# First feed-forward by seven products per pair of weight tiles on mixed halves of two token streams, and the long-convolution filters built in the mixers

## The chip, the cores and the metric

One NeuronCore of one Trainium2 chip runs the whole layer in one launch. The metric is the device time of a run in microseconds (us). The five engines have a queue each and run it in order: TensorE (PE, its weight loads are PEld), VectorE (DVE), ScalarE (ACT), GpSimd (POOL) and SyncE (SP, which here only starts DMAs). A scheduler fixes the order of each queue when the program is built, so an instruction that waits holds up everything behind it on its engine.

## The reference

A diffusion-transformer layer over 512 latent tokens (`x`) and 256 context tokens (`ctx`), width 1024, cut to what matters:

```python
h = half_ffn(h, m[0], m[1], m[2], wg0, wu0, wd0)        # 512 tokens, D_FF = 2816 = 22 tiles of 128
hc = half_ffn(hc, mc[0], mc[1], mc[2], wg0, wu0, wd0)   # 256 tokens, the same weights
n, nc = modulate(rms_norm(h), ...), modulate(rms_norm(hc), ...)
s_fw, s_bw = context_states(nc, w_in, lb)               # gated linear recurrence, final states
out = token_mixers(n, s_fw, s_bw, hyena_kernels(...))   # recurrence heads + long convolutions, gates, w_out
h = half_ffn(h + m[5] * out, m[6], m[7], m[8], wg1, wu1, wd1)
return rms_norm(h) * final_norm_w

def half_ffn(h, shift, scale, gate, wg, wu, wd):
    x = modulate(rms_norm(h), shift, scale)
    return h + 0.5 * gate * ((silu(x @ wg) * (x @ wu)) @ wd)
```

`hyena_kernels` is a small network that makes the filters of the two long convolutions from weights alone. All is float32.

## The kernel before

Tokens lie along the free axis, features on the 128 partitions. A float32 product is three products of halves: `split` (L115) writes a rounded copy `hi` on ACT (L116) and the rest `lo` on DVE (L117), and `mm3` (L242) issues `whi*xhi`, `whi*xlo`, `wlo*xhi` (L244, L245, L247). Weights come as tiles of 128x1024 through three `wraw` buffers on SP's queue and are split into rings `whi` and `wlo` of three buffers each.

**Stage 1, first feed-forward** (`ffn0`, L745). Over four groups of the 22 hidden tiles, each gate or value tile is multiplied with 512 latent columns (`ps_gl`) and 258 context columns (`ps_gc`, two of them carry the shift vectors); then `down` (L443) adds the group's share into the residuals `hl` and `hc`, which stay in SBUF. Two other pieces of work are woven in: `mod_steps` (dot products for the modulation vectors on DVE, their 56 weight tiles `wmod` fetched on POOL's queue) and, through the planner `Clock`, `filters` (L627), which builds the convolution filters with POOL, DVE, ACT and a few products (`ps_w`, `ps_last`, `ps_l`, `ps_k`) and leaves them in `k_dram`.

**Stage 2, mixers.** A list `todo` of 52 pieces of plain projection work is the filler: 12 `hy` (convolution inputs), 4 `g`, 16 `m` (gates), 4 `v`, 12 `z` (inputs of the four recurrence heads) and 4 `pb`, on PE named `ps_w`, `ps_wc`, `ps_v`, `ps_pb`. `Clock.run` steps through a chain of work and, where by its cost model the chain waits on vector work, puts in filler. Chains are `convs` (L1017: four passes, two convolutions by two channel halves, products `ps_e`, `ps_i`, `ps_j` between long sequences of DVE sums and products at L1031) and `head` (L1133: four recurrence heads, two at a time, products `ps_s` and DVE work at L1176 to L1188).

```python
def allowed(f):
    if f[0] == "z":
        return f[1] == 0 or (state["conv"] and f[1] - state["heads"] < 3)
...
ck.run([convs()], fill, lambda i: True)
state["conv"] = True
```

**Stage 3** multiplies by `w_pa` and `w_out`. **Stage 4**, the second feed-forward, forms the gates and values of hidden tiles 4 to 21 pair by pair with seven products of half tiles (`pair_products`, L1350; `ps_p`, 256 columns each) on sums of weight quarters made by `quads` (L176).

Of the kernel before, what the change touches and what calls it, by code (L numbers as in the profile page):

```python
# [10 lines left out]
F32 = mybir.dt.float32  # L11
# [11 lines left out]
T = L + C  # L23
D = 1024
# [3 lines left out]
GROUPS0 = ((0, 6), (6, 12), (12, 17), (17, 22))  # L28
# [53 lines left out]

@with_exitstack
def layer_kernel(ctx: ExitStack, tc: tile.TileContext, a: dict, out: bass.AP):
# [3 lines left out]
    const = ctx.enter_context(tc.tile_pool(name="const", bufs=1))  # L88
    wp = ctx.enter_context(tc.tile_pool(name="wp", bufs=1))
    mx = ctx.enter_context(tc.tile_pool(name="mx", bufs=1))  # L90
    psp = ctx.enter_context(tc.tile_pool(name="psp", bufs=1, space=PSUM))
# [5 lines left out]
    def c8(name, dims, dt=F32):  # L97
        return mx.tile([P] + dims, dt, tag="c8", name=name, bufs=8)
# [7 lines left out]
    def c1(name, dims, dt=F32):  # L106
        return mx.tile([P] + dims, dt, tag="c1", name=name, bufs=7)
# [15 lines left out]
    RING, ONE8, TWO4, QUAD = range(4)  # L123
    hold = lambda x, kinds: [y + (k,) for y, k in zip(x, kinds)]
    plan = []
    for g, (f0, f1) in enumerate(GROUPS0):
        gu = [(a[w][0, ft], 1024) for ft in range(f0, f1) for w in ("wg", "wu")]
        plan += hold(gu[:6], [RING] * 3 + [ONE8] + [TWO4] * 2) + gu[6:] if g == 0 else gu
        down = [(a["wd"][0, dm, :, f0 * P:f1 * P], (f1 - f0) * P) for dm in range(KT)]
        plan += hold(down, [ONE8] * 3 + [RING] * 5) + down[3:6] if g == len(GROUPS0) - 1 else down  # L130
# [27 lines left out]
    def choose():  # L158
        f = next(f for f in todo if allowed(f))
# [47 lines left out]

    def prefetch(ahead=2):
        while wstate["next"] < len(plan) and sum(2 if len(h) == 2 else 1 for h in wstate["held"]) < 2 * ahead:
# [8 lines left out]
            src, cols, *kind = plan[wstate["next"]] or choose()  # L218
            if kind == [QUAD]:
                wstate["quads"] = quads(src, cols)  # L220
                continue
# [3 lines left out]
            if kind == [ONE8]:  # L225
                both = c8("wkeep", [2, 1024], F32R)
                hi, lo = both[:, 0], both[:, 1]
            elif kind == [TWO4]:
# [51 lines left out]
    nhi = const.tile([P, KT, L], F32R, name="nhi")  # L280
    nlo = const.tile([P, KT, L], F32R, name="nlo")

# [36 lines left out]
    junk = c8("junk", [2048])  # L319

    def dot(raw, i, res):
        return V.scalar_tensor_tensor(out=junk[:, 0:1024], in0=raw, scalar=1.0, in1=cvb[:, i], op0=ALU.mult, op1=ALU.mult,  # L322
                               accum_out=res)

    def mod_steps():
        pair = c8("wmod", [2, 1024])
        raw = [pair[:, 0], pair[:, 1], c4("wmod", [1024])]
# [1215 lines left out]
```

## Time and profile before

| | us |
|---|---|
| median of 3 runs (1528.41 to 1530.3) | 1530.17 |
| the profiled execution's own time | 1527.99 |
| its span, first to last instruction | 1526.2 |
| PE busy in the span | 1484.9 |
| DVE busy | 1035.7 |
| ACT busy | 555.7 |
| POOL busy | 305.7 |

Busy time is that in which at least one instruction of an engine is under way. Matmuls overlap in the pipeline, so what one costs is the step from one start to the next, not its own duration. By the starts of its products, stage 1 lasts until 655 us of the span, the convolutions lie between 730 and 884, the heads between 888 and 1078, and stage 4 goes from 1152 to the end.

### The profile page before, as it was taken

How to read it: one execution, taken by the hardware profiler on the slowest of the kernel's cores; microseconds unless marked ns; L12 is line 12 of the kernel's file. 1: busy time of each engine (PE TensorE's matmuls, PEld its weight loads, DVE VectorE, ACT ScalarE, POOL GpSimd, SP SyncE). 2: the span in 40 equal slices, each digit the busy share in tenths (PEclk: the TensorE clock that was granted, in tenths of full speed). 3: DMA queues.
4: the chain of work that ended last, by engine and by line, in shares of the span. 5: the costliest groups of instructions: out<-in, count | busy, mean ns of one | idle time of the engine just before them, and what ended most of it. 6: DMA issues, size and time to landing. Idle time of an engine off the chain costs nothing. (4 is left out here: it accounts for less than half of the span.)

```text
span 1526.2 us, 22141 instructions
## 1 busy us (share of the span) xinstructions
PE 1484.9 (97%) x8776; PEld 1294.7 (85%) x8776; DVE 1035.7 (68%) x1553; ACT 555.7 (36%) x947; POOL 305.7 (20%) x248
## 2 busy tenths in 40 slices
PE   8899999999999999999999999999998999999997
PEld 5698888888888888878888888888798889999896
DVE  7946984475456554675776756875757768769686
ACT  5342112212322232444433324444433435435253
POOL 1400110010254464000000021223431002212020
PEclk9999999999999999999999999999999999999999
DMA  8334674462223333334542421124633142332422
GB/s 333 129 108 135 200 237 148 143 233 94 80 94 99 99 107 99 132 111 138 171 137 93 131 90 49 63 90 152 218 111 94 39 128 85 96 110 88 121 83 84
DMA packets 69704, 188.93 MB, mean 124 GB/s; under 512 B 7835, under 2 KB 16799, under 8 KB 69344
## 3 DMA queue, kind: packets, MB, share of 16 engines
q1 hardware_dynamic: 58608, 152.61, 30.5%
q0 software_dynamic: 9408, 33.70, 6.7%
q8 instruction: 69, 1.13, 0.3%
q10 hardware_dynamic: 1584, 1.20, 0.2%
q14 instruction: 35, 0.29, 0.1%
HBM read 169.92 MB, written 17.56 MB: 123 GB/s over the span
## 5 line engine op out<-in xcount | busy, mean ns | idle before, releaser
L116 ACT CAST whi<-wraw 128x1024 fp32r<-128x1024 f32 (+3 forms) x188 | 171.0, 910 | 489.4 <-PE ps_gc L245 178.5
L117 DVE TENSOR_TENSOR wlo<-wraw,whi 128x1024 fp32r<-128x1024 f32 (+3 forms) x136 | 156.6, 1152 | 138.7 <-ACT whi L116 138.4
L244 PE MATMUL ps_gl<-nhi,whi 128*128 128x512 f32 x360 | 144.5, 401 | 0.0
L244 PE MATMUL ps_w<-nhi,whi 128*128 128x512 f32 x352 | 143.2, 407 | 1.3 <-ACT th L940 1.1
L247 PE MATMUL ps_w<-nhi,wlo 128*128 128x512 f32 x352 | 140.0, 398 | 3.3 <-DVE wlo L117 3.3
L247 PE MATMUL ps_gl<-nhi,wlo 128*128 128x512 f32 x360 | 142.5, 396 | 0.0
L245 PE MATMUL ps_gl<-nlo,whi 128*128 128x512 f32 x360 | 142.1, 395 | 0.0
L245 PE MATMUL ps_w<-nlo,whi 128*128 128x512 f32 x352 | 140.0, 398 | 0.0
L117 POOL TENSOR_TENSOR wlo<-wraw,whi 128x1024 fp32r<-128x1024 f32 x25 | 62.5, 2501 | 383.0 <-ACT whi L116 370.3
L245 PE MATMUL ps_dl<-mid,whi 128*128 128x512 f32 (+1 forms) x321 | 123.7, 386 | 0.0
L247 PE MATMUL ps_dl<-mid,wlo 128*128 128x512 f32 (+1 forms) x321 | 123.6, 387 | 0.0
L244 PE MATMUL ps_dl<-mid,whi 128*128 128x512 f32 (+1 forms) x321 | 123.3, 389 | 0.0
L322 DVE SCALAR_TENSOR_TENSOR junk<-wmod,cvb 128x1024 f32<-128x1024 f32 x80 | 97.7, 1222 | 2.8 <-DMA wmod<-in_mod_w 1.6
L244 PE MATMUL ps_gc<-chi,whi 128*128 128x258 f32 x328 | 93.2, 284 | 5.9 <-ACT chi L116 5.7
L245 PE MATMUL ps_gc<-clo,whi 128*128 128x258 f32 x328 | 94.0, 287 | 0.0
L247 PE MATMUL ps_gc<-chi,wlo 128*128 128x258 f32 x328 | 92.8, 283 | 0.0
L1369 POOL TENSOR_TENSOR u<-p,res 128x512 f32<-128x512 f32 x18 | 33.2, 1847 | 283.7 <-ACT p L1364 140.0
L244 PEld LDWEIGHTS ps_gl<-nhi,whi 128*128 128x128 f32 x360 | 67.5, 187 | 18.5 <-ACT bias L798 0.8
L247 PEld LDWEIGHTS ps_w<-nhi,wlo 128*128 128x128 f32 x352 | 66.5, 189 | 17.5 <-DVE wlo L117 3.7
L244 PEld LDWEIGHTS ps_w<-nhi,whi 128*128 128x128 f32 x352 | 66.7, 190 | 16.3 <-ACT th L940 1.4
L244 PEld LDWEIGHTS ps_gc<-chi,whi 128*128 128x128 f32 x328 | 62.4, 190 | 19.9 <-ACT chi L116 6.2
L332 POOL DMA_DIRECT2D wmod<-in_mod_w x56 | 29.6, 529 | 238.1 <-DVE junk L322 194.6
(460 smaller groups left out, 4102.8 us busy)
## 6 DMA issues: line engine op xcount, KB each, us to landing
wmod<-in_mod_w POOLq DMA_DIRECT2D x56, 512.0 KB, 4.5
wraw<-in_wg SPq DMA_DIRECT2D x44, 512.0 KB, 3.5
wraw<-in_wu SPq DMA_DIRECT2D x44, 512.0 KB, 3.6
wraw<-in_w_in SPq DMA_DIRECT2D x44, 512.0 KB, 3.2
wraw<-in_wd SPq DMA_DIRECT2D x40, 384.0 KB, 3.5
wm<-in_mod_w SPq DMA_DIRECT2D x16, 512.0 KB, 8.0
wraw<-in_wd SPq DMA_DIRECT2D x19, 320.0 KB, 3.3
win<-in_win SPq DMA_DIRECT2D x16, 256.0 KB, 3.4
```

The lines of the kernel that those rows point to most:

```text
L116: A.copy(hi, x)
L117: return eng.tensor_tensor(out=lo, in0=x, in1=hi.bitcast(F32), op=ALU.subtract)
L244: PE.matmul(o, whi, xhi, start=first, stop=False)
L245: PE.matmul(o, whi, xlo, start=False, stop=False)
L247: PE.matmul(o, wlo, xhi, start=False, stop=last)
L322: return V.scalar_tensor_tensor(out=junk[:, 0:1024], in0=raw, scalar=1.0, in1=cvb[:, i], op0=ALU.mult, op1=ALU.mult, accum_out=res)
L332: nc.gpsimd.dma_start(out=raw[i % 3], in_=a["mod_w"][8 * tiles[i][0] + tiles[i][1]])
L1369: G.tensor_tensor(out=u57, in0=p57, in1=res[:, 1:2].broadcast_to([P, 2, 256]), op=ALU.add)
```

## The change

Hidden tiles 4 to 21 of the first feed-forward are taken in pairs. The 1024 input features are cut into two halves, each weight pair into quarters, and the 512 latent and 256 context tokens are cut into halves too: one half of both streams, with one column for the shift and one of zeros, is a block of `HW` = 386 columns. Seven products of a quarter sum with a block or a sum of blocks (`product0`, named `ps_p`, four input tiles by three products by 386 columns) replace the eight of the plain scheme. `token_sums` makes the sums of blocks once; `quads0` makes the weight sums for each pair, and three of the seven halves get their `lo` by an accumulating DMA on POOL's queue that adds the weights from DRAM to a negated `hi`. `pair_products0` puts the results together with two ACT copies, one ACT negation, four DVE sums and three POOL sums.

There are five groups instead of four. The input blocks and their sums take the room of the residuals, so the residuals lie in DRAM: `hl` is stored in `x0_dram`, the shares of the groups are copied out of PSUM by ACT and added up in `y_dram` and `yc_dram` (a store for the first group, accumulating DMAs on POOL's queue for the next three), and the last group loads both again. `mod_steps` fetches through two buffers on SP's queue instead of three on POOL's, and dots the latent vector of the first 24 tiles in two halves. The filter network and `filters` run in stage 2, in front of the convolutions, with the mixers' pieces as filler; no `z` piece is allowed before the convolutions are done. POOL's descriptor ring is 4096 bytes of a partition.

```diff
-GROUPS0 = ((0, 6), (6, 12), (12, 17), (17, 22))
+GROUPS0 = ((0, 4), (4, 8), (8, 12), (12, 16), (16, 22))
...
-        return mx.tile([P] + dims, dt, tag="c8", name=name, bufs=8)
+        whole = mx.tile([P, 2080], dt, tag="c8", name=name, bufs=12)
...
         if f[0] == "z":
-            return f[1] == 0 or (state["conv"] and f[1] - state["heads"] < 3)
+            return state["conv"] and f[1] - state["heads"] < 3
...
+        def both(x, src=None):
+            w = ("whi", "wlo")[wstate["slot"]]
+            wstate["slot"] ^= 1
+            t = wp.tile([P, 2, 512], F32R, tag=w, name=w, bufs=3)
+            if src is None:
+                split(t[:, 0], t[:, 1], x)
+            else:
+                A.copy(t[:, 0], x)
+                A.activation(t[:, 1], t[:, 0].bitcast(F32), AF.Copy, scale=-1.0)
+                nc.gpsimd.dma_start(out=t[:, 1], in_=src, accum_op=ALU.add)
+            return t[:, 0], t[:, 1], None
+
+        yield both(a11, src0[:, 0:512])
+        s1 = total(a21, a22)
+        s2 = total(s1, a11)
+        yield both(s2)
+        yield both(total(a11, a21))
+        yield both(s1)
+        yield both(a12, src0[:, 512:1024])
+        yield both(a22, src1[:, 512:1024])
+        yield both(total(a12, s2))
...
-        raw = [pair[:, 0], pair[:, 1], c4("wmod", [1024])]
+        raw = [c4("wmod", [1024]) for _ in range(2)]
...
-                nc.gpsimd.dma_start(out=raw[i % 3], in_=a["mod_w"][8 * tiles[i][0] + tiles[i][1]])
+                load(raw[i % 2], a["mod_w"][8 * tiles[i][0] + tiles[i][1]])
...
+    def product0(name, x):
+        whi, wlo, _ = weights()
+        p_ = ps(name)
+        for k in range(4):
+            ks = slice(k * P, k * P + P)
+            mm3([p_[:, 0:HW]], whi[:, ks], wlo[:, ks], [x[k]], k == 0, k == 3)
+        return p_[:, 0:HW - 1]
...
+        p1, u2, p7, n5 = (c2(x, [n]) for x in ("p1", "u2", "p7", "n5"))
+        A.copy(p1, product0("ps_p1", [xone(k, 0) for k in range(4)]))
+        V.tensor_tensor(out=u2, in0=product0("ps_p6", tsum[1]), in1=p1, op=ALU.add)
+        A.copy(p7, product0("ps_p7", tsum[2]))
+        G.tensor_tensor(out=res[:, 1, 0], in0=p7, in1=u2, op=ALU.add)
+        A.activation(n5, product0("ps_p5", tsum[0]), AF.Copy, scale=-1.0)
...
                     down(weights(), [x + y for x, y in zip(lx, cx)], [pl, pc[:, 0:C]])
-                    residual(hl, dm, LS, pl, m_lat, 2)
-                    residual(hc, dm, CS_, pc[:, 0:C], m_ctx, 2)
+                    for p_, al, y, n in ((pl, c2, y_dram, L), (pc, c1, yc_dram, C)):
+                        t = al("yt", [n])
+                        A.copy(t, p_[:, 0:n])
+                        if gi == 0:
+                            store(y[:, dm], t)
+                        else:
+                            nc.gpsimd.dma_start(out=y[:, dm], in_=t, accum_op=ALU.add)
                     adv(bg, 2)
...
-    while "net" not in state:
-        ck.fill(fill)
-    ck.run([filters()], fill, lambda i: True)
...
     ck.run([context_norm()], fill, lambda i: True)
     ftab = forward_table()
+    ck.run([filters()], fill, lambda i: True)
     inverse_table(0)
```

The order of the queues at three places. First PE at the first pass of the convolutions, before, behind the pass's last forward product (`ps_e`; `ps_w` is a projection of the filler):

```order
L244 MATMUL ps_e<-zhi,ft 128x256
L245 MATMUL ps_e<-zlo,ft 128x256
L247 MATMUL ps_e<-zhi,ft 128x256
L247 MATMUL ps_w<-nhi,wlo 128x512
L244 MATMUL ps_w<-nhi,whi 128x512
L245 MATMUL ps_w<-nlo,whi 128x512
```

The same place in the changed program:

```order
L316 MATMUL ps_e<-zhi,ft 128x256
L317 MATMUL ps_e<-zlo,ft 128x256
L319 MATMUL ps_e<-zhi,ft 128x256
L316 MATMUL ps_i<-ys,it 128x256 x2
L316 MATMUL ps_e<-zhi,ft 128x256
L317 MATMUL ps_e<-zlo,ft 128x256
```

Before, 130 products of the filler stand between the first pass's forward and inverse products; in the changed program none does. There, 2 inverse products (`ps_i`), 19 forward ones of the next pass, 22 inverse and 5 forward ones follow; the first `ps_w` comes after the fourth pass's forward products, and 46 of them stand ahead of the last `ps_j`.

Second DVE at the same place, before, from the sums of the first pass on (`y`, `x` and `sb` are its operands, `kt` the filter):

```order
L1031 TENSOR_TENSOR y<-x,kt 128x512 x2
L1031 TENSOR_TENSOR x<-x,kt 128x512 x2
L117 TENSOR_TENSOR wlo<-wraw,whi 128x1024
L1031 TENSOR_TENSOR y<-y,x 128x256 x4
L1031 TENSOR_TENSOR x<-y 128x512
```

And in the changed program:

```order
L1225 TENSOR_TENSOR y<-x,kt 128x512 x2
L1225 TENSOR_TENSOR x<-x,kt 128x512 x2
L1225 TENSOR_TENSOR y<-y,x 128x256 x4
L1225 TENSOR_TENSOR x<-y 128x512
L1225 TENSOR_TENSOR x<-sb,x 128x512
```

The splits of filler weights (`wlo`) are gone from here; DVE has the four passes' own work one behind the other.

Third POOL in stage 1 of the changed program, at the end of the second group (`whi` and `wlo` from `in_wg` and `in_wu` are the accumulated weight halves, `g` is a result of seven products); before, POOL's queue held only the 56 `wmod` fetches and the filters' sums here:

```order
L993 DMA y_dram<-yt 128x512 x4
L993 DMA yc_dram<-yt 128x256
L262 DMA wlo<-in_wg 128x512
L262 DMA whi<-in_wg 128x512
L262 DMA wlo<-in_wu 128x512
L889 TENSOR_TENSOR g<-p_2439,u_2438 128x385
L891 TENSOR_TENSOR g<-u_2438,n_2440 128x385
L892 TENSOR_TENSOR g<-n_2440,g 128x385
L262 DMA wlo<-in_wu 128x512
```

Weight halves now stand in one queue behind the additions to `y_dram`, which wait for ACT's copies out of PSUM, and behind the sums of results, which wait for products.

## Rows read from the trace of the kernel before

**Rows 1.** The page's busy times over the whole span (us, share, instructions).
```profile
PE 1484.9 (97%) x8776; PEld 1294.7 (85%) x8776; DVE 1035.7 (68%) x1553; ACT 555.7 (36%) x947; POOL 305.7 (20%) x248
```
**Rows 2.** Windows: from:to, length, PE, PEld, DVE, ACT, POOL busy (instructions), PEclk, DMA share, GB/s.
```profile
80.00:360.00 280.00, 279.81 (x1627) 245.78 (x1626) 182.16 (x302) 66.18 (x117) 29.62 (x56) 1.00 0.52 170
400.00:580.00 180.00, 180.00 (x1010) 150.65 (x1009) 100.31 (x133) 51.36 (x94) 94.75 (x92) 1.00 0.28 90
730.00:884.30 154.30, 153.19 (x801) 129.82 (x800) 113.02 (x186) 52.69 (x77) 2.39 (x1) 1.00 0.41 135
884.30:888.50 4.20, 4.20 (x21) 3.38 (x20) 1.13 (x2) 1.42 (x2) 0.29 (x1) 1.00 0.18 68
888.50:1048.90 160.40, 156.87 (x953) 137.76 (x951) 120.90 (x193) 73.71 (x142) 40.53 (x17) 1.00 0.23 78
1048.90:1078.30 29.40, 29.22 (x155) 24.46 (x156) 13.03 (x21) 12.49 (x28) 8.80 (x4) 1.00 0.65 224
1207.00:1490.00 283.00, 279.15 (x1954) 261.20 (x1953) 220.44 (x299) 126.09 (x205) 51.44 (x36) 1.00 0.33 100
```
**Rows 3.** PE's timeline in stage 1 (start, duration, engine, line, op, tiles, form, count).
```profile
201.01 0.39 PE L244 MATMUL ps_gl<-nhi,whi 128*128 128x512 f32 x1
201.24 0.40 PE L245 MATMUL ps_gl<-nlo,whi 128*128 128x512 f32 x1
201.47 0.28 PE L244 MATMUL ps_gc<-chi,whi 128*128 128x258 f32 x1
...
202.07 0.40 PE L244 MATMUL ps_gl<-nhi,whi 128*128 128x512 f32 x1
```
**Rows 4.** PE's timeline in stage 4, seven-product part, twelve steps apart.
```profile
1310.03 0.28 PE L244 MATMUL ps_p<-nhi,wlo 128*128 128x256 f32 x1
...
1311.47 0.28 PE L244 MATMUL ps_p<-nhi,whi 128*128 128x256 f32 x1
```
**Rows 5.** Groups of DVE between 730 and 884.3 (count, busy us, mean ns, idle before).
```profile
L117 DVE TENSOR_TENSOR wlo<-wraw,whi 128x1024 fp32r<-128x1024 f32 x19 | 23.2, 1223 | 10.4 <-ACT whi L116 10.2
...
L1031 DVE TENSOR_TENSOR x<-ps_e,sb 128x512 f32<-128x512 f32 (+1 forms) x12 | 6.8, 598 | 7.9 <-PE ps_e L247 7.8
...
L1119 DVE TENSOR_TENSOR x2v<-ps_j,x2v 128x256 f32<-128x256 f32 x6 | 3.5, 626 | 12.2 <-PE ps_j L247 12.2
...
L1100 DVE TENSOR_TENSOR x1v<-ps_i,x1v 128x512 f32<-128x512 f32 x4 | 2.8, 692 | 8.3 <-PE ps_i L247 8.3
...
L942 DVE TENSOR_SCALAR KR<-th,lb_n,lbt 128x512 f32<-128x512 f32 (+1 forms) x4 | 1.6, 475 | 0.0
...
L1142 DVE TENSOR_TENSOR kd<-KR 128x512 f32<-128x512 f32 x1 | 0.7, 687 | 0.0
```
**Rows 6.** PE's timeline behind a gap in stage 1, 258 columns each.
```profile
74.62 0.58 PE L244 MATMUL ps_gc<-chi,whi 128*128 128x258 f32 x1 [5.71 <-ACT chi L116]
...
75.68 0.42 PE L244 MATMUL ps_gc<-chi,whi 128*128 128x258 f32 x1
...
78.26 0.42 PE L244 MATMUL ps_gc<-chi,whi 128*128 128x258 f32 x1
```
**Rows 7.** The window that holds these products.
```profile
75.00:80.00 5.00, 5.00 (x29) 4.92 (x29) 0.03 (x1) 0.43 (x1) 0.00 (x0) 0.64 0.00 0
```
**Rows 8.** Groups of PE between 884.3 and 1078.3, one of three lines each.
```profile
L244 PE MATMUL ps_w<-nhi,whi 128*128 128x512 f32 x132 | 54.4, 412 | 0.0
...
L245 PE MATMUL ps_wc<-clo,whi 128*128 128x256 f32 x48 | 13.7, 285 | 0.0
...
L244 PE MATMUL ps_pb<-obhi,whi 128*128 128x512 f32 x32 | 12.8, 416 | 1.2 <-ACT obhi L116 1.2
```
**Rows 9.** The page's group of POOL's fetches (busy us, mean ns).
```profile
L332 POOL DMA_DIRECT2D wmod<-in_mod_w x56 | 29.6, 529 | 238.1 <-DVE junk L322 194.6
```
**Rows 10.** DMA issues: tiles, queue, count, KB each, us to landing.
```profile
wmod<-in_mod_w POOLq DMA_DIRECT2D x56, 512.0 KB, 4.5
...
k_dram<-te POOLq DMA_DIRECT2D x8, 256.0 KB, 2.8
```

More of the change, by code (lines that the diff above doesn't have):

```diff
@@ L23 @@
 T = L + C
+HL, HC = L // 2, C // 2
+HW = HL + HC + 2
 D = 1024
@@ L158, in choose @@
     def choose():
-        f = next(f for f in todo if allowed(f))
+        f = next((f for f in todo if allowed(f)), None)
+        if f is None:
+            return None
         todo.remove(f)
@@ L206, in quads, with quads0, total @@
         yield held(a22)
+    def quads0(src0, src1):
+        raws = []
+        for src in (src0, src1):
+            raws.append(raw_tile("wraw"))
+            load(raws[-1], src)
+        (a11, a12), (a21, a22) = (r.rearrange("p (h c) -> h p c", h=2) for r in raws)
+        def total(x, y):
+            t = c2("qs", [512])
+            V.tensor_tensor(out=t, in0=x, in1=y, op=ALU.add)
+            return t
+        def both(x, src=None):
[18 more added lines that the diff above has]
+        yield both(total(a12, s2))
     def prefetch(ahead=2):
@@ L217, in prefetch @@
                 continue
-            src, cols, *kind = plan[wstate["next"]] or choose()
-            if kind == [QUAD]:
-                wstate["quads"] = quads(src, cols)
+            what = plan[wstate["next"]] or choose()
+            if what is None:
+                return
+            src, cols, *kind = what
+            if kind and kind[0] in (QUAD, QUAD0):
+                wstate["quads"] = (quads if kind == [QUAD] else quads0)(src, cols)
                 continue
@@ L316, in recurrence_bounds, with dot @@
         V.tensor_scalar_mul(out=lb_n1, in0=lb_c1, scalar1=-1.0)
[L319 to L323, printed above, removed]
+    def dot(out_, raw, vec, res):
+        return V.scalar_tensor_tensor(out=out_, in0=raw, scalar=1.0, in1=vec, op0=ALU.mult, op1=ALU.mult, accum_out=res)
+    m_part = const.tile([P, KT], F32, name="m_part")
     def mod_steps():
-        pair = c8("wmod", [2, 1024])
-        raw = [pair[:, 0], pair[:, 1], c4("wmod", [1024])]
+        raw = [c4("wmod", [1024]) for _ in range(2)]
         tiles = [(j, dm) for j in range(2, 9) for dm in range(KT)]
@@ L745, in ffn0, with hidden0 @@
+    def hidden0(pg, pu, bg_, bu, sg, md, mid):
+        A.activation(sg, pg, AF.Silu, bias=bg_)
+        V.scalar_tensor_tensor(out=md, in0=pu, scalar=bu, in1=sg, op0=ALU.add, op1=ALU.mult)
+        split(by2(mid[:, 0]), by2(mid[:, 1]), md)
+        return mid
+    n_c = 2 * (HC + 2)
+    bg = mod_steps()
     def ffn0():
@@ L747, in ffn0 @@
             ml, mc = [], []
-            first = iter(())
             if gi == 0:
@@ L976, in fill_all @@
             prefetch()
+            while not chosen:
+                yield None
+                prefetch()
             f = chosen.pop(0)
```

276 lines of the change are left out of this document (189 added, 87 removed).

## The prediction

> **What bounds the kernel now.** I read the page's busy times first: PE is busy 97% of the span, DVE 68% [rows 1]. Then the windows, stage by stage, because a share over the span says nothing about one stage: PE loses 0.2 us in the 280 us of plain gates and values, nothing where the filters are woven in, 1.1 us in the convolutions, 3.7 us in the heads and 3.9 us in the seven-product part of stage 4 [rows 2]. So PE's queue sets the time in every stage, and less work for PE is worth its full time as long as the rest keeps it fed. What feeds it differs. In the convolutions DVE is busy 113.0 of 154.3 us [rows 2], and idle there mostly because its products stand behind filler in PE's queue (8.3, 12.2 and 7.9 us) [rows 5]: a chain that needs PE little, with projections filling PE's time. That filler is what to watch, since the change spends it elsewhere. Two questions follow: what do the seven products save on PE, and what does PE do once its filler is used up?
>
> **The products (a gain).** One round of three 512-column and three 258-column products takes 202.07 - 201.01 = 1.06 us [rows 3], a weight tile of eight rounds 8.48 us, and the 36 tiles that go over to the new scheme 305.3 us. Per column that is 1.06 / 2310 = 0.459 ns. The new scheme has 18 pairs x 7 products x 12 = 1512 matmuls of 386 columns. No row has that width. At 0.459 ns a column one takes 0.177 us and all 267.8 us; at the rate of 256 columns, (1311.47 - 1310.03) / 12 = 0.120 us or 0.469 ns a column [rows 4], 273.6 us; at that of 512, (201.47 - 201.01) / 2 = 0.23 us or 0.449 ns, 262 us. I take 267.8, as 386 columns lie in the middle of the mix that it is measured on. Two more context columns in 192 remaining products cost 0.2 us. **Term: -37.3 us** (-31 to -43). `down` has the same columns in five groups as in four.
>
> **The filters' move (the largest loss).** Their own work is unchanged and PE was full around it in stage 1 [rows 2], so the filters by themselves cost nothing there or in stage 2; their POOL work, 95 us, goes to a stretch where POOL has little, and their loads and `k_dram` writes move into SP's and POOL's queues between the `w_in` weights, a few of 256 KB at 2.8 us [rows 10]. But in stage 1 their waits were covered by the feed-forward, and now they use up the mixers' pieces. By the order of PE's queue, all `hy`, `g`, `m` and `v` stand ahead of the last filter product, `z` may not start before the convolutions are done, and `pb` needs `z`. The convolutions are left with nothing: no `ps_w` between their products up to the fourth pass, and no `wlo` split on DVE.
>
> How long do the bare convolutions take? DVE's work in the old stretch is 113.0 us [rows 2], less 23.2 for `wlo` and 7.3 for seven groups of other work, from `KR` 1.6 down to `kd` 0.7 [rows 5]: 82.5 us, and 83.6 with two `x2v` products that fell behind the stretch. The four passes stand one behind the other, so that is a floor. At each of three hand-overs DVE waits for products: 2 + 19 + 22 + 5 = 48 matmuls of 256 columns follow the first kept result, 5.8 us at 0.120 [rows 4], with some 6 us of DVE work (three more splits, the sums already possible, `x1v`, `zlo`) beside them. Here the clock comes in. After a gap of 5.71 us PE's next products start 0.215 us apart (75.68 to 78.26, twelve steps) instead of 0.120, and the granted clock of that window is 0.64, partly at the lower of its two levels, 1.2 and 2.4 GHz [rows 6, 7]. Between bursts of the bare convolutions PE idles some 15 us, so each burst starts slow and takes up to 10.3 us. I take 4 us of waiting at each hand-over (between 0 and 4.3, nearer the slow end because the burst begins slow), 3 us before the first sums and 8 us for the last products behind DVE's last split: 83.6 + 12 + 3 + 8 = 106.6, say 107 us. The ends are 92 (all at full clock) and 122 (the 28 us of old waits and 10 for the clock). The Trainium skill, TensorE: Matmul & The Clock Gate, section "Part 1: The HAM clock gate", says that the array's clock falls to half when it idles and that activity releases it again. That agrees with the rows [rows 6, 7]; with the rule the stretch comes out some 12 us longer than at the full clock throughout, so the rule speaks against this change.
>
> PE's work in these 107 us: the convolutions' own 240 matmuls at 0.120 = 28.8 us, and 46 products of the first `z` pieces, about 8 us. So 70 us of PE time are lost where 1.1 were: **+69 us** (52 to 84). Behind the convolutions the queue runs 110 more products of `z`, dense, before the first head can begin.
>
> **The heads (a smaller loss).** PE was busy 4.2 + 156.9 + 29.2 = 190.3 us from 884.3 to 1078.3 [rows 2], of which 396 `ps_w` and 96 `ps_pb` of 512 at 0.234 (1.06 us less three of 256, by three) and 144 `ps_wc` at 0.120 are filler [rows 8]: 132 us, own work 58. The new queue has some 61 us of `z` and 22 of `pb` left here: 141 us with the heads' own 58. DVE's work is 135 us [rows 2], so neither engine now covers the other. Between 141 (perfect overlap) and 175 (DVE only 77% busy, near its 75% of before) I take 155, nearer the good end, since DVE waited mostly on PE's longer queue. 14 us lost against 3.7: **+10 us** (0 to 30).
>
> **Feeding the seven products (a small loss).** Nearest is stage 4, the same scheme at 0.120 us a matmul, which lost 3.9 us of 283 [rows 2]. Here each product takes 12 x 0.177 = 2.1 us instead of 1.4, so its DVE work has more room; but 54 weight halves come by an accumulating DMA that no row shows. Issue is 0.53 us on POOL [rows 9]; landing I bound by 2.8 us for 256 KB and 4.5 for 512 KB [rows 10], the latter the likelier as the transfer reads twice. With two ACT copies of some 0.6 us each the half is ready 6 us after its slot is free, and the ring lets it start at least three products, 6.3 us, ahead. It just fits. Behind a late one in POOL's queue stand the sums of results, for which DVE waits and then PE. **Term +5 us** (0; or half a microsecond for each of 54, 27).
>
> **At nothing:** the copies of partial sums (ACT has 66 us busy in 280 [rows 2]) and their additions in DRAM; POOL's weight halves stand behind those, covered by the first four products of a group, 8 us, and if they are late their cost is in the term above. The 56 `wmod` loads now pass through SP's queue, each waiting for DVE's dot products with weight loads and result stores queued behind; DVE is busy 182 of 280 us there [rows 2], and the cover, one pair of weight tiles, is 14.9 us long. DVE's second sum per residual of the last group stands beside `down`.
>
> **Sum.** -37.3 + 69 + 10 + 5 = +46.7 us on a span of 1526.2: 1572.9, and with the 1.8 us around the span 1574.7. The median shown is 2.2 us above the profiled execution. **Forecast 1575 us.** From the bounds: 1537 with all at their best, 1638 with all at their worst; all at one end is unlikely, and I give this case by itself 1553 to 1600.
>
> **Rivals.**
> - *The clock stays low through the convolutions and the thin part of the heads.* For: bursts of 48 products, about 10 us at the slow step. Against: the row shows full pace again after 4 us of products. Price: the heads' 58 us of small products partly doubled, +20: 1595. Chance 0.12.
> - *The accumulated weight halves come late.* For: three steps on three engines and a transfer, with 0.3 us to spare by my count. Against: DVE's four halves in between give POOL time. Price 27 instead of 5: 1597, and from 1 us each on 1624. In the Trainium skill, SBUF — State Buffer, section "SBUF: two separate sides", DMAs started by GpSimd wait while VectorE holds a shared port, as their descriptors are written by software. The trace has no sign of it: 56 fetches took 0.53 us each at DVE's 65% [rows 2, 9]. Chance 0.11.
> - *The convolutions cost little without filler (the other side).* If their stretch is mainly PE's queue and not DVE's work, it shrinks. The point that decides: with 22 us lost there (stretch 59 us) the change is even; at 45 us it gives 1513. For: DVE idled 28 us in it behind filler. Against: 82.5 us of DVE work by rows. Chance 0.07.
> - *The change saves no PE time*, because a matmul of 386 columns is bounded by its weight load. Against: 256 columns already run at 0.120 us with a load each [rows 4]. 1612. Chance 0.04.
>
> **The numbers.** The forecast's case has 0.66. The range 1540 to 1610 takes in the clock, most of late weights and both tails of the main case, and leaves out the other side, the worst of late weights and no saving. Below 0.2%, 3 us, no difference can be told from none. Faster: 0.05 of the other side; same: the remaining 0.02 of it and 0.01 of the main case's tail; slower 0.92.
>
> **What would show it.** Right: `ps_p` of 386 columns 0.177 us apart with PE full in stage 1; the filters' stretch full; then 100 us or more from first to last convolution product in which PE is busy under half and its granted clock is below 1 in pieces, DVE over 75%. Wrong: gaps before `ps_p` released by DMA or POOL; filler products among `ps_e` and `ps_i`; a stretch under 75 us; or heads that take as long as before with PE half idle.

## The result and the profile after

The changed kernel takes 1681.56 us (median of 4 runs, 1675.28 to 1685.26) against 1529.29 us for the kernel before on the same chip: ratio 1.0993, 95% interval 1.0969 to 1.1017. It is 152 us slower; the forecast was 1575 us and the range ended at 1610. The sign was right, the size a third of what came. The profiled execution has a span of 1673.5 us, 147.3 us more than the 1526.2 of before, and all sums below are made on these two spans.

The page's busy times after, to be read against [rows 1]:

```profile
PE 1489.9 (89%) x8560; PEld 1328.3 (79%) x8560; DVE 1150.2 (69%) x1814; ACT 670.9 (40%) x1196; POOL 429.3 (26%) x353
```

PE has 216 products fewer in the records, is busy about as long as before, and idles 183.6 us instead of 41.3: 142.3 us more. Its work fell by 37.3 us, yet its busy time rose by 5.0, so by this estimate some 42 us of it are what products at a low clock took beyond their time at the full one. The windows by stage, which answer to [rows 2] (from:to, length, busy time of PE, PEld, DVE, ACT and POOL with instructions, PEclk, DMA share, GB/s):

```profile
119.80:651.30 531.50, 474.02 (x2594) 442.91 (x2593) 356.56 (x618) 232.69 (x444) 154.03 (x158) 0.94 0.69 181
651.00:727.00 76.00, 66.81 (x288) 54.20 (x287) 45.26 (x72) 28.33 (x43) 0.00 (x0) 0.93 0.40 131
726.90:928.40 201.50, 201.50 (x911) 156.79 (x911) 103.21 (x118) 70.45 (x104) 103.75 (x95) 1.00 0.44 145
928.40:1034.20 105.80, 47.84 (x289) 44.63 (x288) 92.64 (x160) 18.66 (x30) 14.67 (x13) 0.69 0.24 82
1034.20:1226.10 191.90, 171.94 (x1020) 152.22 (x1018) 134.44 (x223) 82.01 (x166) 47.04 (x20) 0.93 0.25 83
1226.10:1673.50 447.40, 428.18 (x2952) 399.21 (x2952) 328.79 (x470) 182.82 (x304) 75.25 (x46) 0.98 0.31 97
```

In order: stage 1 from its first `down` to its last, the first mixer projections, the filters, the convolutions, the heads with the `z` products ahead of them, and stages 3 and 4. Two stretches inside these, one of the pairs in stage 1 and the heads behind the `z` products:

```profile
240.00:270.00 30.00, 30.00 (x173) 26.54 (x172) 18.85 (x39) 10.25 (x22) 8.08 (x10) 1.00 0.67 169
1054.80:1226.10 171.30, 151.34 (x910) 134.53 (x908) 123.84 (x213) 74.66 (x154) 39.84 (x17) 0.93 0.24 81
```

The convolutions (PE 45% busy, clock 0.69) are as foretold. Stage 1, where PE lost 0.2 us in 280 before, now idles 57.5 us. What PE waits for there, from the view of its waits between 153 and 660 us (line, releaser: us in total, times, longest):

```profile
PE ps_p L316 <- ACT wlo L142: 26.3, 4, 21.6
PE ps_sum L459 <- DVE acc L451: 13.4, 1, 13.4
PE ps_p L319 <- DMA whi<-in_wg: 5.7, 5, 1.8
PE ps_p L319 <- DVE wlo L143: 4.5, 2, 3.8
PE ps_p L319 <- DMA whi<-in_wu: 3.2, 3, 2.3
```

There are three different things in it. **First, the modulation's dot products.** PE's timeline at the change from `down` to the first pair:

```profile
154.22 0.34 PE L316 MATMUL ps_p<-bh,whi 128*128 128x386 f32 x1
...
155.63 0.34 PE L319 MATMUL ps_p<-bh,whi 128*128 128x386 f32 x1
177.60 0.69 PE L316 MATMUL ps_p<-tt,wlo 128*128 128x386 f32 x1 [21.62 <-ACT wlo L142]
```

The eight steps from 154.22 to 155.63 are 0.176 us each, the price that the forecast took. Then PE waits 21.62 us for ACT's copy of a sum of weight quarters, and ACT waits for the two additions on DVE that make this sum. DVE's timeline meanwhile (`L392` is a dot product, `L250` the first of the additions):

```profile
164.88 0.69 DVE L392 SCALAR_TENSOR_TENSOR junk<-wmod,cvb 128x512 f32<-128x512 f32 x1 [0.70 <-DMA wmod<-in_mod_w]
...
171.64 0.69 DVE L392 SCALAR_TENSOR_TENSOR junk<-wmod,cvb 128x512 f32<-128x512 f32 x1 [1.23 <-DMA wmod<-in_mod_w]
...
174.99 0.69 DVE L250 TENSOR_TENSOR qs<-wraw 128x512 f32<-128x512 f32 x1
```

From 164.88 to 171.64 two modulation steps pass, 3.4 us each: 2.7 us of dot products and a wait for the next row of `mod_w` in one of two buffers. Sixteen of them go with the eight `down` tiles of a group, 54 us, and `down` of the first group takes 33.5 us. Those left over stand ahead of the additions in DVE's queue.

**Second, the residuals.** SP's timeline in the last group (issue of DMAs), and DVE's beside it:

```profile
604.76 0.33 SPq L139 DMA_DIRECT2D h_dram<-hl  x1
605.13 0.43 SPq L136 DMA_DIRECT2D xr<-x_dram  x1
605.60 0.46 SPq L136 DMA_DIRECT2D yr<-y_dram  x1
610.91 0.32 SPq L139 DMA_DIRECT2D h_dram<-hl  x1
```

```profile
609.40 0.69 DVE L1001 TENSOR_TENSOR yr<-ps_dl,yr 128x512 f32<-128x512 f32 x1 [3.28 <-DMA yr<-y_dram]
610.13 0.75 DVE L1002 SCALAR_TENSOR_TENSOR hl<-yr,m_lat,xr 128x512 f32<-128x512 f32 x1
```

The store of a finished tile waits in SP's queue for DVE; the loads of the next tile's residual and partial sum stand behind it; DVE waits for them; its result releases the next store. One turn of this ring takes 610.91 - 604.76 = 6.15 us, while the 18 latent products of `down` take 4.2. After eight tiles `ps_sum` comes 13.4 us late.

**Third, the weight halves that come by an accumulating DMA.** Times to landing, from the page's DMA issues (form, count, KB each, us):

```profile
wmod<-in_mod_w SPq DMA_DIRECT2D x56, 512.0 KB, 6.0
y_dram<-yt POOLq DMA_DIRECT2D x24, 256.0 KB, 8.1
whi<-in_wg POOLq DMA_DIRECT2D x18, 256.0 KB, 7.3
wlo<-in_wu POOLq DMA_DIRECT2D x18, 256.0 KB, 5.0
yr<-y_dram SPq DMA_DIRECT2D x8, 256.0 KB, 3.5
```

The weight halves land in 5.0 to 7.3 us where the forecast had 4.5 as the likelier bound from [rows 10], and the `wmod` rows take 6.0 instead of 4.5 [rows 10].

### The profile page after: what moved, and what is told of

It reads as the page before. It is cut to its first block, busy times and chain, and to the rows that moved or that the text cites. A ratio compares the mean times of both kernels' runs of the same rounds, so it can differ in the third digit from the quotient of the medians.

```text
span 1673.5 us, 22809 instructions
## 1 busy us (share of the span) xinstructions
PE 1489.9 (89%) x8560; PEld 1328.3 (79%) x8560; DVE 1150.2 (69%) x1814; ACT 670.9 (40%) x1196; POOL 429.3 (26%) x353
## 4 chain that ended last, share of the span: by engine, by line
PE 62%; DVE 17%; DMA 11%; issue 5%; ACT 2%; POOL 2%; SPq 0%; ACTq 0%; DVEq 0%; POOLq 0%
PE ps_p L319 6%; PE ps_p L316 6%; PE ps_p L317 6%; PE ps_w L316 5%; PE ps_w L317 5%; PE ps_w L319 5%; DMA wmod<-in_mod_w 4%; PE ps_dl L316 3%; PE ps_dl L317 3%; PE ps_dl L319 3%; DVE x L1225 2%; DVE wlo L143 1%; DVE wmod L392 1%; PE ps_s L1362 1%; DMA yr<-y_dram 1%
## 5 line engine op out<-in xcount | busy, mean ns | idle before, releaser
L142 ACT CAST whi<-wraw 128x1024 fp32r<-128x1024 f32 (+2 forms) x160 | 134.5, 842 | 297.3 <-issue 88.2
L143 DVE TENSOR_TENSOR wlo<-wraw,whi 128x1024 fp32r<-128x1024 f32 (+2 forms) x111 | 114.1, 1031 | 88.6 <-ACT whi L142 86.5
L392 DVE SCALAR_TENSOR_TENSOR wmod<-wmod,cvb 128x1024 f32<-128x1024 f32 x56 | 68.6, 1229 | 31.4 <-DMA wmod<-in_mod_w 31.0
L319 PEld LDWEIGHTS ps_w<-nhi,wlo 128*128 128x128 f32 x352 | 67.9, 193 | 15.4 <-DVE wlo L143 2.8
L317 PEld LDWEIGHTS ps_w<-nlo,whi 128*128 128x128 f32 x352 | 68.2, 194 | 11.6
L319 PE MATMUL ps_p<-bh,whi 128*128 128x386 f32 x180 | 63.5, 354 | 8.9 <-DMA whi<-in_wg 5.7
L142 ACT CAST whi<-qs 128x512 fp32r<-128x512 f32 x72 | 44.1, 620 | 63.8 <-DVE qs L250 24.4
L316 PEld LDWEIGHTS ps_dl<-mid,whi 128*128 128x128 f32 x318 | 59.6, 188 | 11.8 <-ACT mid L142 0.2
L319 PEld LDWEIGHTS ps_dl<-mid,wlo 128*128 128x128 f32 x318 | 60.0, 189 | 7.1
L317 PEld LDWEIGHTS ps_dl<-mid,whi 128*128 128x128 f32 x318 | 59.8, 188 | 7.1
L143 DVE TENSOR_TENSOR wlo<-qs,wlo 128x512 fp32r<-128x512 f32 x72 | 54.9, 773 | 11.8 <-ACT wlo L142 11.5
L319 PE MATMUL ps_p<-bh,wlo 128*128 128x386 f32 x180 | 61.9, 344 | 1.1 <-DMA wlo<-in_wg 1.0
```

Of the source, the lines that this page charges most:

```text
L142: A.copy(hi, x)
L143: return eng.tensor_tensor(out=lo, in0=x, in1=hi.bitcast(F32), op=ALU.subtract)
L316: PE.matmul(o, whi, xhi, start=first, stop=False)
L317: PE.matmul(o, whi, xlo, start=False, stop=False)
L319: PE.matmul(o, wlo, xhi, start=False, stop=last)
L392: return V.scalar_tensor_tensor(out=out_, in0=raw, scalar=1.0, in1=vec, op0=ALU.mult, op1=ALU.mult, accum_out=res)
```

## The experiments

All were timed beside the kernel before on the same chip; its medians there lie between 1528.80 and 1529.48. Differences are between medians, against 1681.56 for the changed kernel, whose runs spread by 10 us. A few microseconds are therefore nothing, and where little is at stake the profile decides.

### The filters' move alone

`b1_filters` is the kernel before with one part of the change:

```diff
-            return f[1] == 0 or (state["conv"] and f[1] - state["heads"] < 3)
+            return state["conv"] and f[1] - state["heads"] < 3
...
-    ck.run([filters()], fill, lambda i: True)
...
     ck.run([context_norm()], fill, lambda i: True)
+    ck.run([filters()], fill, lambda i: True)
```

> The kernel before with one part of the change alone: the filters are built in the mixers instead of beside the first feed-forward, and the `z` projections wait for the convolutions as in the changed kernel; the first feed-forward keeps its products. Theory A (the mixers' loss belongs to the filters' move alone, 67 us in the convolutions, 25 in the heads and a few between as the marks of the changed kernel show): slower than before by 85 to 105 us, to some 1625, with convolutions of about 106 us. Rival B (part of that loss is made by the seven products' pools, queues or late ends): slower by less than 65 us.

Measured: 1602.23 us, ratio 1.0477 (1.0460 to 1.0494), 73.0 us slower than before: between the two. To see where, I set against each other, for each stage, the time between its marks in PE's timeline and PE's work in it (the products in PE's queue at 0.120, 0.177 and 0.232 us for 256, 386 and 512 columns, the others by a rough count). What is left over is "lost". The count is too low for small products: with these on the line through the three prices, the start has 6 us more work and the heads 14, in all three kernels alike. So each stage holds a constant, and only differences mean anything.

```
                                before             b1_filters         after
                                us    work  lost   us    work  lost   us    work  lost
start, to the first ps_dl       145.2 107.7  37.5  146.4 107.7  38.7  119.8  74.0  45.8
stage 1 and filters, to ps_e    585.0 555.7  29.3  701.7 672.3  29.5  808.6 695.1 113.5
convolutions                    154.1 152.5   1.6  116.0  63.4  52.6  105.8  36.9  68.9
heads, to the first ps_pa       194.0 148.9  45.1  192.0 121.4  70.6  191.9 121.4  70.5
stages 3 and 4                  447.9 418.9  29.0  447.2 418.9  28.3  447.4 418.9  28.5
```

The filters cost nothing where they are now built (29.5 us lost against 29.3), but the convolutions lose 51 us more than before and the heads 25: the move alone is worth half of the result. The ban on `z` pieces ahead of the convolutions is part of this run and was not tried by itself. The convolutions lost less than the 67 us that I took from the changed kernel because 35 us of filler were left for them. In `b1_filters` the small network that the filters come from still runs in stage 1.

### The network

`e8_net` takes that network out of the mixers of the changed kernel again:

```diff
-        for _ in filter_net():
-            yield 0.4, 3.0
...
+            net = filter_net()
             for dm in range(KT):
...
                 sq_add(acc, hk(hl2, dm), dm, c2, L)
+                adv(net)
```

> In the changed kernel the small network of the filters (two sine layers, masks, its last table) runs beside the last group of the first feed-forward, as in the kernel before, and only the filters themselves stay in the mixers. Theory A (the network's chain, during which PE has little of its own to do, uses up 27 us of filler products that the convolutions then lack): the convolutions begin some 27 us sooner, last about 10 us longer with filler in them, and the time falls by 10 to 20 us. Rival B (the network's DVE work lands on the loop of residuals, which is late already): the gap before `ps_sum` grows, and the time falls by less than 5 us or rises.

Measured: 1661.74 us, ratio 1.0872 (1.0856 to 1.0889), 19.8 us less: theory A. The windows of its filters and its convolutions:

```profile
658.30:904.50 246.20, 237.87 (x1077) 188.16 (x1076) 132.69 (x169) 86.36 (x131) 97.18 (x92) 0.98 0.42 143
904.50:1018.70 114.20, 75.39 (x402) 67.11 (x401) 99.38 (x162) 26.16 (x40) 22.68 (x16) 0.79 0.31 104
```

The first is 31 us shorter than in the changed kernel (277.1 from the last `down` to `ps_e`), the second 8 us longer and as in `b1_filters`, and the last `down` comes 7 us later (658.3 instead of 651.3). A chain in which PE has almost nothing of its own used up 27 us of filler.

### More filler for the convolutions, or for the heads

`e4_held` keeps twelve `m` pieces back until the filters are done; `e10_heads` keeps four until the convolutions are done:

```diff
+        if f[0] == "m" and f[1] >= 4:
+            return state["filt"]
```

```diff
+        if f[0] == "m" and f[1] >= 12:
+            return state["conv"]
```

> Twelve of the sixteen mixer projections `m` are held back until the filters are built, so 66 us of filler products move from the filters' stretch into that of the convolutions; no arithmetic is changed. Theory A (the convolutions lose 69 us only because their filler was spent beside the filters, which need less of it): the convolutions' stretch stays near 106 us but with PE full, the filters' stretch shrinks by 50 to 66 us, and so does the time, to some 1620. Rival B (the filters' own chain on POOL and DVE is as long as their stretch of 200 us): the loss moves into the filters and the time falls by less than 20 us.

> In the changed kernel four `m` projections (22 us of PE) are held back from the filters' stretch until the convolutions are done, so that they stand among the heads. Theory A (the heads take 192 us by a chain of their own through PE, DVE and ACT, whether 132 or 104 us of filler stand in them; the term for the heads was too small by the filler that left): the heads stay within 6 us of 192, the filters' stretch gets shorter by some 20, and the time falls by 12 to 22 us. Rival B (PE's queue sets the heads): they get longer by 15 to 22 us and the time stays within 5 us.

Measured: `e4_held` 1676.22 us, ratio 1.0961 (1.0938 to 1.0983), 5 us less; `e10_heads` 1684.27 us, 1.1021 (1.1004 to 1.1039), 3 us more. For `e4_held` rival B holds. Its windows of the filters and of the convolutions:

```profile
731.00:913.30 182.30, 141.80 (x624) 109.80 (x623) 97.11 (x110) 53.10 (x80) 92.61 (x94) 0.84 0.34 115
913.30:1035.10 121.80, 106.55 (x569) 92.23 (x569) 102.25 (x168) 35.18 (x53) 18.09 (x14) 0.94 0.41 139
```

With 67 us less filler the filters' stretch gets only 19 us shorter and PE idles 40 us in it, 38.0 of them for POOL's sums of absolute values, as its waits say:

```profile
PE ps_l L799 <- POOL hw L790: 38.0, 2, 20.6
```

The convolutions, with PE busy 106.55 of 121.80 us again, get 16 us longer. In `e10_heads` the heads:

```profile
1037.50:1235.90 198.40, 185.99 (x1125) 163.71 (x1123) 141.47 (x222) 89.94 (x176) 58.37 (x24) 0.99 0.28 97
```

24 us more filler, 6.5 us more time, half a microsecond over what theory A allows. By these two points the heads' stretch fits a chain through PE, DVE and ACT of some 192 us, beside which PE's queue begins to bind at 128 us of filler. In the changed kernel PE's longest waits among the heads are for ACT:

```profile
PE ps_ot L1437 <- ACT on L1431: 12.0, 4, 3.4
```

That half of theory A holds. The other half does not: the filters' stretch did not shrink (205.7 us), and a wait for POOL took the filler's place.

```profile
PE ps_l L799 <- POOL hw L790: 24.4, 1, 24.4
```

So three stretches stand one behind the other in the mixers, and in the two moves tried, filler moved from one to another only moved the hole. That the filters' stretch is a chain of fixed length is not shown, though. The products `ps_l` that end the four quarters of the filters start at 794.2, 838.5, 873.3 and 904.1 us in `e4_held`: the last two quarters, which have no filler left, take 35 and 31 us. In `e10_heads` they start at 791.3, 838.5, 882.8 and 925.2. Its last quarter takes 42 us. In ACT's queue there, splits of filler weights stand ahead of the quarter's own work (`hw`) and wait for their loads, the last one for 7.34 us:

```profile
917.90 1.04 ACT L142 CAST whi<-wraw 128x1024 fp32r<-128x1024 f32 x1 [7.34 <-DMA wraw<-in_w_in]
918.85 0.62 ACT L781 ACTIVATE hw<-hw 128x512 f32<-128x512 f32 x1
```

So the preparation of filler lengthens the filters' stretch that the filler is meant to cover. Another order of it was not tried.

### The clock in the convolutions

`e7_busy` gives PE products that nothing reads in the gaps of the bare convolutions, so it has more work than the changed kernel:

```diff
+                busy = ps("ps_busy")
+                for n in range((85, 65, 33, 22)[2 * o + hh]):
+                    PE.matmul(busy, zhi[:, n % 4, 0:P], zhi[:, 0], start=True, stop=True)
```

> In the changed kernel, behind each pass of forward products of the convolutions PE is given 85, 65, 33 and 22 products of 512 columns whose result nothing reads, at 0.233 us each a little less than the gaps of 22.2, 17.0, 9.3 and 7.0 us. Theory A (PE's clock falls in these gaps and makes the products behind them slow, as the granted clock of 0.70 shows): PE's clock stays near 1 in the stretch, and the convolutions get 8 to 15 us shorter. Rival B (the slow products stand beside DVE work anyway): the clock is high but the stretch and the time stay within 4 us.

Measured: 1682.45 us, ratio 1.0999 (1.0983 to 1.1016), no difference: rival B. The window of its convolutions:

```profile
933.20:1039.80 106.60, 90.99 (x494) 79.45 (x493) 93.34 (x161) 19.99 (x32) 14.85 (x13) 0.92 0.24 81
```

The granted clock rises from 0.69 to 0.92 and the stretch stays at 106 us. DVE is busy 93 of them either way. The edit has two effects on DVE that offset each other. Its idle time before the products at the hand-overs (the last column), first in the changed kernel, then in `e7_busy`:

```profile
L1225 DVE TENSOR_TENSOR x<-ps_e,sb 128x512 f32<-128x512 f32 (+1 forms) x12 | 6.8, 594 | 2.0 <-PE ps_e L319 2.0
L1294 DVE TENSOR_TENSOR x1v<-ps_i,x1v 128x512 f32<-128x512 f32 x4 | 2.8, 692 | 3.9 <-PE ps_i L319 3.9
```

```profile
L1225 DVE TENSOR_TENSOR x<-ps_e,sb 128x512 f32<-128x512 f32 (+1 forms) x12 | 6.8, 592 | 0.5 <-PE ps_e L319 0.5
L1297 DVE TENSOR_TENSOR x1v<-ps_i,x1v 128x512 f32<-128x512 f32 x4 | 2.8, 691 | 3.2 <-PE ps_i L319 3.2
```

They fall from 5.9 to 3.7 us, but the added products then make DVE wait 2.6 us for a `ps_j` for which it did not wait before. So the low clock is mostly a consequence here: what a higher one gives back at the hand-overs is some 2 us of the 106.

### Stage 1's three losses

`e1_dots` and `e5_spread` move modulation steps. The first:

```diff
-                    adv(bg, 2)
+                    adv(bg, 1 if gi == 0 else 2)
```

The second has one step behind each `down` product of every group, and four in a pair of tiles:

```diff
         A.copy(p7, product0("ps_p7", tsum[2]))
+        adv(bg)
...
+        adv(bg)
         return res
```

> One line of the changed kernel is altered: behind each of the eight `down` products of the first group the modulation advances by one step instead of two (the 8 steps left over go to later groups, which have room for them). Theory A (16 dot-product steps at 3.4 us each do not fit beside 33.5 us of `down`, stand ahead of the sums of weights in DVE's queue, and so hold the first `ps_p` of a sum for 21.6 us, after which PE's clock is low): the wait at 156 us is gone and the time falls by 20 to 30 us, to some 1655. Rival B (the first pair's weights are late because they come by an accumulating DMA behind other transfers): the wait stays, and the time is within 5 us of 1681.6.

> The 56 modulation steps of the changed kernel are spread: one behind each `down` product instead of two, and four in each pair of tiles (behind the third and the last of each seven products) instead of one. Theory A (too many dot products of 3.4 us stand in a block at each change from `down` to a pair): the gaps of 21.6, 3.4 and 3.8 us before `ps_p` go, no gap of over 4 us takes their place, and the time falls by 20 to 35 us. Rival B (DVE has no room for them in the pairs either, or the loads through SP's queue hold the weights): the gaps turn up within the pairs, and the time falls by less than 10 us.

`e1_dots`: 1674.94 us, ratio 1.0956 (1.0938 to 1.0974), 7 us less where theory A had 20 to 30. The wait at 156 us is gone, but the long steps that were put off now pile up at the next change, and PE's timeline there has

```profile
282.70 0.69 PE L316 MATMUL ps_p<-tt,wlo 128*128 128x386 f32 x1 [29.62 <-ACT wlo L142]
```

The mechanism is theory A's, the edit was too small for it. `e5_spread`: 1657.66 us, ratio 1.0841 (1.0823 to 1.0859), 23.9 us less. No wait of over 4.1 us is left before `ps_p`. What shows in their place are the accumulated halves, from its waits:

```profile
PE ps_p L319 <- DMA whi<-in_wg: 14.2, 8, 4.1
```

`e2_store` takes the residual's store out of the ring, `e3_split` has DVE split all seven weight tiles:

```diff
-                store(h_dram[:, dm], hk(hl2, dm))
+                nc.gpsimd.dma_start(out=h_dram[:, dm], in_=hk(hl2, dm))
```

```diff
-        yield both(a11, src0[:, 0:512])
+        yield both(a11)
...
-        yield both(a12, src0[:, 512:1024])
-        yield both(a22, src1[:, 512:1024])
+        yield both(a12)
+        yield both(a22)
```

> The store of each finished residual tile to `h_dram` in the last group is issued from POOL's queue instead of SP's; nothing else is changed. Theory A (in SP's queue the store waits for DVE's residual, and the loads of the next tile's partial sum and residual stand behind it, so that one tile takes 6.1 us in a ring of store, load, landing and DVE, against 4.2 us of PE's `down`): the 13.4 us gap before `ps_sum` and the low clock behind it go, and the time falls by 12 to 25 us. Rival B (the partial sums are late because the additions in DRAM end late, or the landing itself of 3.5 us is the cost): within 4 us of 1681.6.

> The three weight halves of each pair that came by an accumulating DMA are split on DVE like the other four (54 more subtractions of 512 columns, about 0.69 us each, 37 us of DVE in all; the 54 transfers, the negated copies on ACT and their POOL issues are gone). Theory A (the accumulated halves come late, 9.9 us of PE's gaps in all are released by them): the time falls by 5 to 15 us. Rival B (DVE is the tighter engine in the pairs, as it is busy 77 % there): the gaps before `ps_p` released by DVE grow and the time rises by 5 to 25 us.

`e2_store`: 1667.44 us, ratio 1.0914 (1.0889 to 1.0939), 14.1 us less, and the gap before `ps_sum` falls from 13.4 to 4.7 us:

```profile
PE ps_sum L459 <- DVE acc L451: 4.7, 1, 4.7
```

`e3_split`: 1669.70 us, ratio 1.0919 (1.0897 to 1.0941), 11.9 us less. No gap before `ps_p` is released by a DMA any more, where 9.9 us were. Those released by DVE do not grow; those that end with ACT's `whi` grow from 1.9 to 4.8 us. Theory A in both. Then all three together:

> Three edits in one: the residual's store on POOL's queue, all weight halves split on DVE, and the modulation steps spread. Theory A (three separate losses of stage 1): the gains add up, 14 and 12 us measured and 20 to 35 for the third, so 45 to 60 us less than the changed kernel, some 1628. Rival B (they share one cause, DVE's lack of room, so that more splits on DVE and dot products in the pairs collide): at most 25 us less.

1633.84 us, ratio 1.0690 (1.0672 to 1.0708): 47.7 us less, against 49.9 for the sum of the single gains. They are separate losses. PE is still idle in stage 1 for 22.4 of 488.9 us:

```profile
118.50:607.40 488.90, 466.49 (x2594) 438.64 (x2593) 384.01 (x673) 200.85 (x390) 117.93 (x112) 0.98 0.55 167
```

The largest wait left there is again one for a sum of weights:

```profile
PE ps_p L316 <- ACT wlo L142: 8.3, 3, 7.2
```

### Everything that helped

`e9_net_held` joins the three repairs, the network in stage 1 and the twelve `m` pieces held back; `e11_start` adds one edit at the start:

```diff
-            if kt in (0,1,3,4,5,7):
+            if kt in (0,1,3):
                 pool_dot(shift_w[kt], m0[:, kt, 1:2])
```

> The three repairs of stage 1 (store on POOL's queue, all halves split on DVE, modulation steps spread), the filters' network beside the last group, and twelve `m` projections held back until the filters are built. Theory A (without the network the filters need less filler than they got, so what is held back fills the convolutions): some 10 to 20 us from the network and 15 to 30 from the filler on top of the 1633.8 of the repairs alone, so 1585 to 1610. Rival B (the filters' chain still lasts about 180 us, the loss only moves into it): above 1612.

> The version before it (three repairs, network beside the last group, twelve `m` held back) with one more edit at the start: of the eight shift rows of the first modulation, DVE now makes both dot products for five and POOL and ACT for three, instead of two and six. Theory A (the context's first product waits 14 us, against 5.7 in the kernel before, because six rows pass through POOL's 2.4 us products one behind the other in three buffers that the loads wait for): the wait falls by 4 to 8 us, the first `ps_dl` comes at 114 to 118 instead of 122, and the time is 1594 to 1598. Rival B (DVE is as late there, its own work slowed beside POOL's): the wait stays within 3 us and so does the time, at 1599 to 1605.

`e9_net_held`: 1601.84 us, ratio 1.0474 (1.0456 to 1.0491), 32 us less than the repairs alone: theory A. The network alone gave 20 of these in `e8_net`; if it does so here, some 12 are the filler's. `e11_start`: 1599.42 us, ratio 1.0469 (1.0444 to 1.0495). The context's wait falls from 14.6 to 10.5 us and the first `ps_dl` comes at 115.8 instead of 122.4, both as theory A has it, but the time does not: 2.4 us of median cannot be told from nothing. The best version is 70 us slower than the kernel before. Nothing tried points to one that beats it.

## Why the prediction was wrong

By the table above the miss of 1673.5 - 1572.9 = 100.6 us falls into four pieces: +87.5 in stage 1, its start and the filters' stretch (8.3 + 84.2 lost, where 5 were priced), +15.4 in the heads, -1.7 in the convolutions, -0.5 behind them.

**The products: right.** The step is 0.176 us, PE's work fell by 37.3 us, and the stretch from 240 to 270 us is full, as are others of the pairs. The rivals "no PE saving" and "the other side" fell.

**The filters' own place: right.** PE is busy 201.50 of 201.50 us in their stretch. Their price stands elsewhere, as the forecast said.

**The bare convolutions: right in sum, wrong inside.** 105.8 us against 107, 67.3 us lost against 69. But DVE's work is 92.6 us, not 83.6. Of the 9 us of excess, 1.7 are the tail of the last filter, whose last products DVE still does when the first convolution's begin. Another 5 are convolution products that take longer while POOL still works on that filter beside them:

```profile
934.07 2.35 DVE L1225 TENSOR_TENSOR x<-x 128x512 f32<-128x512 f32 x2
936.45 3.30 DVE L1225 TENSOR_TENSOR y<-x,kt 128x512 f32<-128x512 f32 x2
```

```profile
935.82 1.71 POOL L809 TENSOR_TENSOR te<-ep,to 128x512 f32<-128x512 f32 x1
937.49 1.70 POOL L809 TENSOR_TENSOR tw<-te,tw 128x512 f32<-128x512 f32 x1
```

A product of 512 columns takes 1.65 us there. Its group of DVE in the convolutions, in the kernel before and in the changed one (count, busy us, mean ns, idle before):

```profile
L1031 DVE TENSOR_TENSOR y<-x,kt 128x512 f32<-128x512 f32 x12 | 7.9, 688 | 0.1
```

```profile
L1225 DVE TENSOR_TENSOR y<-x,kt 128x512 f32<-128x512 f32 x12 | 9.9, 852 | 0.1
```

The Trainium skill, SBUF — State Buffer, section "SBUF: two separate sides", says that DVE with both inputs in SBUF and a GpSimd instruction that reads SBUF take turns at a shared pair of ports, each holding it for its whole length. The equal pace, 1.65 beside POOL's 1.70, agrees; alone, POOL's sum of this form took 1.29 us (at 802.80). On the other side DVE waits 13 us instead of the 23 that I summed: 5.9 at the three hand-overs where I had 12, 5.9 before the last products where I had 8, and nothing to speak of before the first sums where I had 3. Of the 12 us that I put down to the clock, `e7_busy` shows some 2. What the Trainium skill says of the clock (TensorE: Matmul & The Clock Gate, section "Part 1: The HAM clock gate") agrees with the granted 0.69; that it speaks against this change by 12 us, as I wrote, does not hold, since most of the slow products stand beside DVE's chain.

**The heads: the step "neither engine now covers the other ... I take 155" failed.** I bounded the stretch by PE's work and DVE's work, 141 to 175 us behind the `z` products, and took a value near the good end. It took 171.3, and with the `z` products 191.9 where 194.0 were before: 28 us of filler were gone, and 2 us of time. 25.4 us were lost instead of 10. The first half of the forecast's own sign for "wrong" came, heads that take as long as before; PE is not half idle in them, but busy 151.34 of 171.30 us. The windows of before could have told: DVE is busy 75% of the heads' stretch and PE nearly always [rows 2], which fits a chain that is as long as PE's queue just as well as two engines that overlap.

**"Feeding the seven products +5" and "at nothing": the steps that failed most.** Each wait inside the stage was named, and each was priced away. For the `wmod` loads I gave as cover one pair of tiles in a plain stretch and DVE's 182 of 280 us; but sixteen steps are tied to the eight `down` tiles of a group, and the change makes groups of four tiles, so `down` of the first group shrank from 50 us (145.2 to 195.5 in the kernel before) to 33.5 while the steps, with two buffers instead of three, took 54. Measured: 24 us. "DVE's second sum per residual stands beside `down`" counted the sum and not the loads that it needs, in a queue in which they stand behind a store: 14 us. The accumulated halves "just fit" by 0.3 us with a landing of 4.5 us; it is 5.0 to 7.3: 12 us, in the lower half of the rival's 27. At the start, which the forecast does not treat, the context's first product waits 14.5 us instead of 5.71 [rows 6]. The loads for its modulation (`cvb`, then the shift rows) are issued from 41.6 us on instead of 31.2, and three shift rows instead of four go at once. This is read from the traces; the one edit tried won 4 us of the 9 that the wait had grown, and no time that can be told from nothing. Of 92.5 us lost in stage 1, its start and the filters' stretch, the runs took back 48 with the three repairs. The rest is some 36 us beside the start. In `e6_repairs` PE still idles 30.6 us between the first `ps_dl` and `ps_e`, where 3.5 were before, behind sums of weights, the norm's sums and the context's residuals; what is left after that fits the low clock behind each gap. No run takes these apart.

**The range.** It held one bad case at a time. But even the sum with every bound at its worst, 1638, ends 44 us short of the result, and the terms that had bounds stayed within them: the convolutions 67.3 in 52 to 84, the heads 25.4 in 0 to 30, the weight halves 12 in 0 to 27. What broke the range is what stood at nothing and so had no bound: the modulation steps, the residuals' loads, the start, and the remainder above. That the change fills the slack of DVE and of two queues on which the "nothings" rested fits the first two; but the gains of the repairs add up, so they are separate losses and not one.

## What to carry to other kernels

- Work that another stage covers has a price only when it moves. Before moving it, add up the lengths of the chains that will then stand one behind the other. If filler must cover all of them and does not suffice, the excess is lost; moving filler about brought little back here (5 us less and 3 us more by itself, some 12 less with the network gone too).
- Background steps tied to a loop's iterations must be spread anew when the loop gets shorter. Count them against the shortest group, at the pace of the buffers they come through.
- A load behind a store in an in-order queue waits for what the store waits for. If that result needs the load of the next iteration, the queue has become a ring, and its turn, not the engines' work, sets the pace.

## What was not expected of the hardware

- PE's low clock cost next to nothing in the convolutions: with 0.69 or 0.92 granted, the stretch is 106 us.
- DMAs that add into their destination land late in this kernel: 5.0 to 7.3 us after issue for 256 KB into SBUF, 8.1 into DRAM, where a plain load of 256 KB (`yr`) takes 3.5. How much of it is other traffic is not shown.
- DVE's products go from 0.69 to 1.65 us beside POOL's sums, and these from 1.29 to 1.70.
- The changed kernel's runs spread by 10 us (1675.28 to 1685.26), those of the kernel before by 3.
